# The scan's thirteen slots divided among KR, BK and Ar; loads issued three units ahead; M loaded through SyncE's queue

## The chip, the cores and the metric

One core of a Trainium2 chip runs the whole network once. The metric is the device time of one execution in microseconds; the median of the runs counts.

## The reference

Two layers, each half-SwiGLU, token mixer, half-SwiGLU, with adaptive RMS norms around them, on 512 latent tokens after 256 context tokens, width 1024, all in float32. The mixer of the first layer is HGRN2, that of the second RWKV-7. The change touches the scan of the RWKV-7 mixer alone, 16 heads of 64, in both directions:

```python
def step(s, inp):
    dec, kt, vt, kkt, bt = inp[:5]
    sa = jnp.einsum('bhvk,bhk->bhv', s, kkt)
    s = s * dec[:, :, None, :] - sa[..., None] * bt[:, :, None, :] + vt[..., None] * kt[:, :, None, :]
    y = jnp.einsum('bhvk,bhk->bhv', s, inp[5]) if with_out else None
    return s, y
...
s_fin, y = lax.scan(step, s0, xs, reverse=reverse)
```

The context is scanned first; the latent scan of the same direction starts from its final state.

## The kernel before, in words

The scan is done in chunks of 64 tokens. Work is cut into twelve units `(qd, g)`: four groups `qd` of four heads, and for each three stretches `g` of 256 tokens (0 is the context, 1 and 2 are the latent tokens), both directions at once. Each unit passes these steps:

- `prep_a` (L1225): loads `hw`, `kk` and `r` (tile KR, one per direction, L1243) and `ld` (L1246); decay matmuls `sw` (L1251), their cumulative sums `cum` (L1264), exponentials on ScalarE; VectorE scales KR in place (L1278) and makes BK from `ld` (L1281); TensorE multiplies BK with KR (L1304), VectorE masks the products into N and, where g is over 0, Ar (L1310); one N is transposed into NT (L1315), and N and NT are stored to a DRAM scratch `md` in eight pieces (L1318).
- `prep_m` (L1323): GpSimd loads M from `md` by its own queue (L1330), inverts 64 triangular 32 by 32 blocks in 30 steps of a product (L1336) and a sum (L1337), and stores the inverse to `me` (L1340).
- `prep_d` (L1344): SyncE loads the inverse in eight pieces into the diagonal blocks P (L1350).
- `prep_b` (L1352): SyncE loads VU (L1359); TensorE transposes BK into `bkt` (L1367, recorded on the helper's line L295), ScalarE copies it to BKT (L1368); matmuls W (L1380).
- `prep_c` (L1386): VectorE transposes P into PT (L1391); matmuls TT and Yo (L1409, L1411) join the diagonal blocks to inverses of 64 by 64.
- `scan` (L1430): four chunks in a row, each with matmuls kG from KR (L1447), `rhs` on VectorE (L1449), matmuls U (L1456), matmuls G from VU and BKT (L1466) and the new state G on VectorE (L1471, L1472), and where g is over 0 the output y from Ar and KR (L1482, L1484).
- `readout` after every third unit (L1497): norm, bonus and gate of two blocks of 128 channels, on TensorE, VectorE and ScalarE.

SBUF tiles of these steps come from rings: a tile takes a free slot of its tag, and what fills it waits until the last reader of the slot's former tile is through. KR, BK and Ar (two each in a unit) share thirteen slots in the pool B1; so do N, NT and M until the pool B2 is open. After that N, NT, M, BKT, W and PT share fifteen slots of B2 (`Q`, L1192).

The order of the instructions on each engine is fixed when the program is built: a scheduler simulates the engines and picks, of what is ready, the instruction that comes first in the program; `urgent` moves a step forward by 400 or 800 places. `rwkv_scan` writes the program's order with generators: the scan of unit i leads, and after each of its yields run three steps of the inversions, five of the preparation and 0.3 of a readout (RM, RP, RO). The preparation is the chain `SEQ = 'Adabc'` (L1556 to L1559): the first two steps of `prep_a` of unit i+2 (A), `prep_d` of i+1 (d), the rest of `prep_a` (a), `prep_b` and `prep_c` of i+1 (b, c). `prep_d` yields until the inversion of i+1 has been written down. Every load and store of the scan but those of M and `me` goes through SyncE's queue, which issues in order: a load that waits for its slot holds up everything behind it. Ahead of the loop a prologue runs beside the value projection (L1544): `prep_a` of unit 0, then the first inversion beside `NPRO` = 12 steps of `prep_a` of unit 1.

Of the kernel before, what the change touches and what calls it, by code (L numbers as in the profile page):

```python
# [9 lines left out]
F32 = mybir.dt.float32  # L10
# [13 lines left out]
I32 = mybir.dt.int32  # L24
RMS_EPS = 1e-6
GN_EPS = 64e-5
NQ1, NQ2 = 13, 15
RM, RP, RO, RV, RF = 3.0, 5.0, 0.3, 1.5, 1.3
NPRO = 12
ORDERED = {mybir.EngineType.PE, mybir.EngineType.DVE, mybir.EngineType.Activation}  # L30
LO = True
RX = 0.12
# [15 lines left out]
NBA, NBS, NB = 2, 4, 2  # L48
TCKW = dict(schedule_with_timeline_sim=True)
HP = 800, 400, 800  # L50
SEQ = 'Adabc'
Q1 = ("KR", "BK", "Ar")


V_NORM = 0
# [18 lines left out]
def trunk(ctx, tc, io, phases=None, dump=None):  # L74
    nc = tc.nc
    act, dve, pool, pe = nc.scalar, nc.vector, nc.gpsimd, nc.tensor
# [8 lines left out]
    def open_pool(name, side="left", **kw):  # L85
        cm = tc.tile_pool(name=name, bufs=1, side=side, reuse_waits="tile", **kw)
        opened[name] = cm
        return cm.__enter__()
# [45 lines left out]
    def urgent(gen, by):  # L134

        while True:
            with tc.high_priority(offset=by):
                x = next(gen, 0)
                if x == 0:
                    return  # L140
            yield x

    def both(*gens):

        gens = list(gens)
        while gens:
            for f in list(gens):
                if next(f, 0) == 0:
                    gens.remove(f)
                else:  # L150
                    yield
# [1029 lines left out]
    def rwkv_scan(l):  # L1181
        nonlocal work, wt, hpool, psw
        B1 = open_pool("B1")
# [6 lines left out]
        late = {}  # L1190

        def Q(name):  # L1192
            first = "B2" not in late or name in Q1
            return (B1 if first else late["B2"]).tile([128, 1024], F32, tag="Q", name=name, bufs=NQ1 if first else NQ2)

        turn = cycle(range(NB))

        def bank(name, tag="b"):

            own, n = {"a": ("a", NBA), "s": ("s", NBS), "b": ("b", 4 - NBA)}[tag]  # L1200
            in_s = tag == "s"
            if tag == "b" and "PS" in late and 4 - NBS and next(turn) == 0:
                in_s, n = True, 4 - NBS
            return (late["PS"] if in_s else PP).tile([128, 512], F32, tag=own, name=name, bufs=n)
# [20 lines left out]
        def prep_a(qd, g):  # L1225
# [7 lines left out]
            KR, BK, N, Ar = ([None, None] for _ in range(4))  # L1233
# [3 lines left out]
            for d in range(2):  # L1237
                t0 = starts(g)[d]
                kr = Q("KR")[:, :1024]
                KR[d] = kr.rearrange("p (s c n) -> p c s n", s=2, n=64)  # L1240
                src = lambda a: a[2 * qd:2 * qd + 2, :, t0:t0 + 256].rearrange("e p t -> p e t")
                for i, nm in enumerate(("kk", "r")[:1 + lat]):
                    nc.sync.dma_start(out=kr[:, 512 * i:512 * i + 512].rearrange("p (e t) -> p e t", e=2), in_=src(S[nm]))  # L1243
                ld = B1.tile([128, 2, 2, 256], F32, tag="L", name="ld", bufs=2)
                for i in range(2):
                    nc.sync.dma_start(out=ld[:, i], in_=src(S[f"bk{d}"][i]))  # L1246
                lds.append(ld)

                p = bank("sw", "a")
                for m in range(2):  # L1250
                    pe.matmul(p[:, 256 * m:256 * m + 256], hw[:, d, 128 * m:128 * m + 128],  # L1251
                              low[qd][:, d], start=True, stop=True)
                sg = B1.tile([128, 512], F32, tag="sg", name="sg", bufs=2)
                act.activation(sg, p, AF.Tanh, scale=0.5)
                dve.tensor_scalar(sg, sg, 0.5, 0.5, ALU.mult, ALU.add)
                sgs.append(sg)
                yield
# [12 lines left out]
            for d in range(2):  # L1270
# [5 lines left out]
                for i, o in ((0, ex), (1, inc))[:1 + lat]:  # L1276
                    x = KR[d][:, :, i]
# [38 lines left out]
            md = dram.tile([64, 32, 32], F32, tag="md", name="md", bufs=2)  # L1316
            for d, hp, b, l0, r0 in lanes:
                nc.sync.dma_start(out=md[l0:l0 + 8].rearrange("l s t -> s l t"),  # L1318
                                  in_=(N[0] if d == 0 else NT_)[r0:r0 + 32, 8 * hp:8 * hp + 8, 32 * b:32 * b + 32])
# [3 lines left out]
        def prep_m(qd, g):  # L1323

            while (qd, g) not in ready:
                yield
            md = ready[qd, g][-1]
            me = dram.tile([64, 32, 32], F32, tag="me", name="me", bufs=2)
            M = Q("M")[0:64, :1024].rearrange("l (s t) -> l s t", t=32)
            pool.dma_start(out=M, in_=md)  # L1330
            eng = ME
            mt = B1.tile([64, 256], F32, tag="mt", name="mt", bufs=2)
            for j in range(30, 0, -1):
                n = 31 - j
                t = mt[:, :j * n].rearrange("l (a b) -> l a b", b=n)
                eng.tensor_tensor(t, M[:, 0:j, j:j + 1].to_broadcast([64, j, n]), M[:, j:j + 1, j + 1:32].to_broadcast([64, j, n]), ALU.mult)  # L1336
                eng.tensor_tensor(M[:, 0:j, j + 1:32], M[:, 0:j, j + 1:32], t, ALU.add)  # L1337
                yield
            eng.memset(M.rearrange("l s t -> l (s t)")[:, 0:1024:33], 1.0)
            pool.dma_start(out=me, in_=M)  # L1340
            inverse[qd, g] = me
            yield
# [154 lines left out]
        def readout(qd, yb, sink):  # L1497

            def one(e):
                j, y = 2 * qd + e, yb[:, e]  # L1500
                ro = lambda n: late["B2"].tile([128, TL], F32, tag="ro", name=n, bufs=3) if qd < 3 else Q(n)[:, :TL]
                bv, g, q = ro("bvl"), ro("gl"), ro("q")
                nc.sync.dma_start(out=bv, in_=S["bv"][j])
                nc.sync.dma_start(out=g, in_=S["g"][j])
                yield
                p = bank("mean")
                pe.matmul(p, blk128, y, start=True, stop=True)
                dve.scalar_tensor_tensor(y, p, -1.0 / 64, y, ALU.mult, ALU.add)
                act.activation(q, y, AF.Square)
                yield  # L1510
                yield
                pq = bank("var")
                for c in range(4):
                    pe.matmul(pq[:, 2 * c:2 * c + 2], q[:, c * 128:c * 128 + 128], blk2, start=True, stop=True)
                rs = rsqrt(pq[:, :8], 8, 1.0 / 64, GN_EPS)
                act.activation(q.rearrange("p (c n) -> p c n", n=64), rs.unsqueeze(2).to_broadcast([128, 8, 64]), AF.Copy)
                yield
                yield
                pr = bank("rsb")
                for c in range(4):  # L1520
                    turned(pr[:, c * 128:c * 128 + 128], q[:, c * 128:c * 128 + 128], TR & 8)
                dve.tensor_tensor(y, y, pr, ALU.mult)
                act.activation(y, y, AF.Identity, scale=vcol(V_LNW, j), bias=vcol(V_LNB, j))
                yield
                dve.tensor_tensor(y, y, bv, ALU.add)
                dve.tensor_tensor(y, y, g, ALU.mult)
                sink(j, y)
                yield

            if qd < 3:  # L1530
                yield from one(0)
                yield from one(1)
            else:
                yield from both(one(0), one(1))
# [5 lines left out]
        none = out = iter(())  # L1540
        stage = lambda f, i: f(*todo[i]) if i < len(todo) else none
        second = prep_a(*todo[1])

        def prologue():  # L1544
            yield from prep_a(*todo[0])
            yield from both(prep_m(*todo[0]), islice(second, NPRO))

# [4 lines left out]
        for _ in both(second, chain(prep_d(*todo[0]), prep_b(*todo[0]), prep_c(*todo[0]))):  # L1552
            pass
        inversions = chain(*(prep_m(*k) for k in todo[1:]))
        for i, k in enumerate(todo):
            ahead = stage(prep_a, i + 2)  # L1556
            ahead = urgent(ahead, HP[1])
            parts = {"A": islice(ahead, 2), "a": ahead, "b": stage(prep_b, i + 1), "c": urgent(stage(prep_c, i + 1), HP[2]), "d": urgent(stage(prep_d, i + 1), HP[2])}
            prep = chain(*(parts[x] for x in SEQ))  # L1559
            due = [0.0] * 3  # L1560
            for _ in urgent(scan(*k, *ready.pop(k)), HP[0]):
                for n, (f, r) in enumerate(((inversions, RM), (prep, RP), (out, RO))):
                    due[n] += r
                    while due[n] >= 1.0:
                        due[n] -= 1.0
                        next(f, None)
            for _ in prep:
                next(inversions, None)
            if k[1] == 2:
                for _ in out:  # L1570
                    pass
                out = readout(k[0], state["y"], to_dram)
# [55 lines left out]
    if on("f00"):  # L1628
# [4 lines left out]
        prep = blocks(0, 0, T, True)  # L1633
# [30 lines left out]
    if on("f10"):  # L1664
# [3 lines left out]
        prep = blocks(1, 0, T)  # L1668
# [3 lines left out]
    if on("mix1"):  # L1672
        prep = squares(T)
# [88 lines left out]
```

## Time and profile before

| | us |
|---|---|
| median of 3 runs | 3894.08 (3892.76 to 3901.19) |
| the profiled execution | 3901.05 |
| its span | 3899.3 |
| TensorE busy | 3551.6 |
| VectorE busy | 2529.3 |
| GpSimd busy | 1382.0 |
| ScalarE busy | 1310.4 |

The profile is of one execution, and its times (us from the start of its span) are those of that execution. A group of instructions is shown by source line, engine, operation and tiles (out<-in). Engines are PE (TensorE matmuls), PEld (its weight loads), DVE (VectorE), ACT (ScalarE), POOL (GpSimd) and SP (SyncE); a q behind the name is the engine's queue, which issues DMAs. A float32 matmul appears as two instructions. What ended a wait is inferred from semaphores: where the engine named had long been done, it was another, often a DMA. The clock of TensorE is given as the granted share of 2.4 GHz, and it takes two levels, 1.00 and 0.50.

### The profile page before, as it was taken

Reading aid. Unit: us, or ns where it says so; the run is one execution under the profiler, and the core shown is the slowest. Engines: PE = TensorE matmul, PEld = TensorE weight load, DVE = VectorE, ACT = ScalarE, POOL = GpSimd, SP = SyncE. Lnnn points to the kernel's source line nnn. Section 1 sums busy time; section 2 is a strip of 40 time slices with the busy share of each in tenths; the row PEclk is TensorE's granted clock in tenths of the full one; section 3 lists DMA queues with packets and bytes.
Section 4 is the critical chain, followed back from the end, with each engine's and each line's share of the span. In section 5 each row is a group of like instructions: output and inputs, shape, how many; then the busy total and the mean of one; then the engine's idle time right before and its main releaser. Section 6 shows DMA issues by size and latency. Waiting matters only on the chain. (4 is left out here: it accounts for less than half of the span.)

```text
span 3899.3 us, 61645 instructions
## 1 busy us (share of the span) xinstructions
PE 3551.6 (91%) x24898; PEld 3115.9 (80%) x24898; DVE 2529.3 (65%) x4042; ACT 1310.4 (34%) x2024; POOL 1382.0 (35%) x1395
## 2 busy tenths in 40 slices
PE   5999998899999899999899999698978889889998
PEld 3898997688888688888799998576867777668887
DVE  6766667656666866666766675776444554468886
ACT  4332333232322432333532333354322222244343
POOL 4212213433433422122422221522366766523332
PEclk9999999999999899999999999798967776779999
DMA  5332331411112233333132332247633332233332
GB/s 186 115 96 88 97 98 44 114 43 44 39 44 66 66 113 103 103 110 113 52 95 82 90 95 78 66 155 240 164 88 81 83 82 63 61 106 91 94 93 81
DMA packets 517051, 362.52 MB, mean 93 GB/s; under 512 B 83517, under 2 KB 490333, under 8 KB 516766
## 3 DMA queue, kind: packets, MB, share of 16 engines
q1 hardware_dynamic: 513694, 350.19, 30.5%
q0 software_dynamic: 1920, 6.29, 0.7%
q8 instruction: 196, 3.21, 0.3%
q10 hardware_dynamic: 1152, 2.10, 0.2%
q14 instruction: 89, 0.73, 0.1%
HBM read 315.64 MB, written 42.87 MB: 92 GB/s over the span
## 5 line engine op out<-in xcount | busy, mean ns | idle before, releaser
L607 PE MATMUL po<-g,whi 128*128 128x512 f32 (+1 forms) x2464 | 593.4, 350 | 10.2 <-ACT g L211 10.2
L551 POOL TENSOR_TENSOR raw<-raw 128x512 f32<-128x512 f32 x88 | 124.9, 1419 | 1341.3 <-DMA raw<-in_ffn_w_in 772.4
L534 PE MATMUL c<-u,whi 128*128 128x386 f32 (+1 forms) x2112 | 524.5, 332 | 48.1 <-DVE uu L565 15.9
L526 ACT ACTIVATE whi<-raw 128x1024 fp32r<-128x1024 f32 x352 | 332.5, 950 | 570.4 <-PE po L607 306.9
L607 PEld LDWEIGHTS po<-g,whi 128*128 128x128 f32 x2464 | 406.2, 190 | 84.6 <-issue 11.4
L527 DVE TENSOR_TENSOR wlo<-raw,whi 128x1024 fp32r<-128x1024 f32 x352 | 416.4, 1187 | 32.3 <-ACT whi L526 30.6
L534 PEld LDWEIGHTS c<-u,whi 128*128 128x128 f32 x2112 | 371.6, 191 | 76.2 <-ACT u L446 25.1
L534 PE MATMUL a<-u,whi 128*128 128x386 f32 (+1 forms) x1408 | 347.4, 331 | 23.6 <-DVE u L428 17.2
L607 PE MATMUL po<-g,wlo 128*128 128x512 f32 (+1 forms) x1232 | 367.1, 348 | 0.0
L611 DVE SCALAR_TENSOR_TENSOR h<-po,mod,h 128x512 f32<-128x512 f32 (+1 forms) x384 | 228.3, 628 | 194.3 <-PE po L607 194.2
L534 PE MATMUL b<-u,whi 128*128 128x386 f32 (+1 forms) x1408 | 344.1, 329 | 2.3 <-ACT pp L562 1.4
L534 PE MATMUL c<-u,wlo 128*128 128x386 f32 (+1 forms) x1056 | 344.9, 327 | 0.0
L534 PEld LDWEIGHTS a<-u,whi 128*128 128x128 f32 x1408 | 251.8, 192 | 29.0 <-issue 18.4
L196 ACT ACTIVATE whi<-raw 128x1024 fp32r<-128x1024 f32 (+1 forms) x193 | 184.7, 959 | 266.8 <-PE c L534 108.5
L534 PEld LDWEIGHTS b<-u,whi 128*128 128x128 f32 x1408 | 246.5, 189 | 12.3 <-issue 6.6
L197 POOL TENSOR_TENSOR wlo<-raw,whi 128x1024 fp32r<-128x1024 f32 x48 | 127.0, 2647 | 302.7 <-ACT whi L196 284.1
L534 PE MATMUL a<-u,wlo 128*128 128x386 f32 (+1 forms) x704 | 233.1, 331 | 0.5 <-DVE wlo L527 0.5
L607 PEld LDWEIGHTS po<-g,wlo 128*128 128x128 f32 x1232 | 208.0, 190 | 29.8
L534 PE MATMUL b<-u,wlo 128*128 128x386 f32 (+1 forms) x704 | 229.2, 326 | 1.0 <-DVE wlo L527 1.0
L1336 POOL TENSOR_TENSOR mt<-M 64x168 f32<-64x168 f32 (+5 forms) x360 | 191.7, 533 | 67.6 <-DMA M<-md 41.2
L1337 POOL TENSOR_TENSOR M<-M,mt 64x168 f32<-64x168 f32 (+5 forms) x360 | 199.6, 555 | 26.4
L534 PEld LDWEIGHTS c<-u,wlo 128*128 128x128 f32 x1056 | 203.5, 193 | 0.0
(362 smaller groups left out, 7295.2 us busy)
## 6 DMA issues: line engine op xcount, KB each, us to landing
raw<-in_ffn_w_in SPq DMA_DIRECT2D x176, 512.0 KB
raw<-in_mod_w SPq DMA_DIRECT2D x144, 512.0 KB
raw<-in_ffn_w_out SPq DMA_DIRECT2D x80, 384.0 KB
raw<-in_hgrn_w_in SPq DMA_DIRECT2D x40, 512.0 KB
raw<-in_ffn_w_out SPq DMA_DIRECT2D x28, 512.0 KB
raw<-in_w_rkv SPq DMA_DIRECT2D x24, 512.0 KB
ld<-s_bk SPq DMA_DIRECT2D x48, 256.0 KB
s_bk<-knb SPq DMA_DIRECT2D x32, 192.0 KB
```

What stands on the lines that cost most here:

```text
L196: act.activation(hi[:, :m], raw[:, :m], AF.Copy)
L197: slots["lo"].tensor_tensor(lo[:, :m], raw[:, :m], hi[:, :m].bitcast(F32), ALU.subtract)
L526: act.activation(hi, x, AF.Copy)
L527: dve.tensor_tensor(lo, x, hi.bitcast(F32), ALU.subtract)
L534: pe.matmul(p[:, :q], a[:, c], x[k][:, b], start=first and k == 0 and i == 0, stop=k == 3 and i == 2, skip_group_check=not first)
L551: pool.tensor_tensor(S[:, lo], U[:, lo], U[:, hi], ALU.add)
L607: pe.matmul(p[v][:, :t1 - t0], wx[:, k, at:at + 128], x[:, e, t0:t1], start=k == 0 and i == 0, stop=k == nk - 1 and i == 2)
L611: dve.scalar_tensor_tensor(h[d][:, t0:t1], p[v][:, :t1 - t0], mods[l, sub, 2][:, d, v:v + 1], h[d][:, t0:t1], ALU.mult, ALU.add)
L1336: eng.tensor_tensor(t, M[:, 0:j, j:j + 1].to_broadcast([64, j, n]), M[:, j:j + 1, j + 1:32].to_broadcast([64, j, n]), ALU.mult)
L1337: eng.tensor_tensor(M[:, 0:j, j + 1:32], M[:, 0:j, j + 1:32], t, ALU.add)
```

## The change

The thirteen shared slots become three rings: 6 for KR, 3 for BK, 4 for Ar. Before the pool B2 is open, N takes slots of Ar's ring, NT and M of KR's. The loads of `prep_a` become a step of their own, ahead of the decay of both directions. In the loop of unit i the order becomes: loads of unit i+3, the decay steps of i+2, `prep_b` and `prep_d` of i+1, the rest of `prep_a` of i+2, `prep_c` of i+1. The prologue takes 10 steps of `prep_a` of unit 1 in place of 12, and the loads of unit 2 are written ahead of the loop. M is loaded by SyncE instead of GpSimd.

```diff
@@ -24,9 +24,9 @@
 I32 = mybir.dt.int32
 RMS_EPS = 1e-6
 GN_EPS = 64e-5
-NQ1, NQ2 = 13, 15
+RINGS, NQ2 = {"KR": 6, "BK": 3, "Ar": 4}, 15
 RM, RP, RO, RV, RF = 3.0, 5.0, 0.3, 1.5, 1.3
-NPRO = 12
+NPRO = 10
 ORDERED = {mybir.EngineType.PE, mybir.EngineType.DVE, mybir.EngineType.Activation}
 LO = True
 RX = 0.12
@@ -48,8 +48,6 @@
 NBA, NBS, NB = 2, 4, 2
 TCKW = dict(schedule_with_timeline_sim=True)
 HP = 800, 400, 800
-SEQ = 'Adabc'
-Q1 = ("KR", "BK", "Ar")
 
 
 V_NORM = 0
@@ -1190,8 +1188,13 @@
         late = {}
 
         def Q(name):
-            first = "B2" not in late or name in Q1
-            return (B1 if first else late["B2"]).tile([128, 1024], F32, tag="Q", name=name, bufs=NQ1 if first else NQ2)
+            if name not in RINGS:
+                if "B2" in late:
+                    return late["B2"].tile([128, 1024], F32, tag="Q", name=name, bufs=NQ2)
+                ring = "Ar" if name == "N" else "KR"
+            else:
+                ring = name
+            return B1.tile([128, 1024], F32, tag=ring, name=name, bufs=RINGS[ring])
 
         turn = cycle(range(NB))
 
@@ -1245,6 +1248,8 @@
                 for i in range(2):
                     nc.sync.dma_start(out=ld[:, i], in_=src(S[f"bk{d}"][i]))
                 lds.append(ld)
+            yield
+            for d in range(2):
 
                 p = bank("sw", "a")
                 for m in range(2):
@@ -1327,7 +1332,7 @@
             md = ready[qd, g][-1]
             me = dram.tile([64, 32, 32], F32, tag="me", name="me", bufs=2)
             M = Q("M")[0:64, :1024].rearrange("l (s t) -> l s t", t=32)
-            pool.dma_start(out=M, in_=md)
+            nc.sync.dma_start(out=M, in_=md)
             eng = ME
             mt = B1.tile([64, 256], F32, tag="mt", name="mt", bufs=2)
             for j in range(30, 0, -1):
@@ -1552,11 +1557,12 @@
         for _ in both(second, chain(prep_d(*todo[0]), prep_b(*todo[0]), prep_c(*todo[0]))):
             pass
         inversions = chain(*(prep_m(*k) for k in todo[1:]))
+        third = stage(prep_a, 2)
+        next(third)
         for i, k in enumerate(todo):
-            ahead = stage(prep_a, i + 2)
-            ahead = urgent(ahead, HP[1])
-            parts = {"A": islice(ahead, 2), "a": ahead, "b": stage(prep_b, i + 1), "c": urgent(stage(prep_c, i + 1), HP[2]), "d": urgent(stage(prep_d, i + 1), HP[2])}
-            prep = chain(*(parts[x] for x in SEQ))
+            ahead, third = urgent(third, HP[1]), stage(prep_a, i + 3)
+            b, c, d = stage(prep_b, i + 1), urgent(stage(prep_c, i + 1), HP[2]), urgent(stage(prep_d, i + 1), HP[2])
+            prep = chain(islice(third, 1), islice(ahead, 4), b, d, ahead, c)
             due = [0.0] * 3
             for _ in urgent(scan(*k, *ready.pop(k)), HP[0]):
                 for n, (f, r) in enumerate(((inversions, RM), (prep, RP), (out, RO))):
```

## Rows read from the trace of the kernel before

**Rows 1.** The profile page: the span, the engines' busy time, and the 40 slices of 97.5 us (the granted clock of TensorE alone).

```profile
span 3899.3 us, 61645 instructions
...
PE 3551.6 (91%) x24898; PEld 3115.9 (80%) x24898; DVE 2529.3 (65%) x4042; ACT 1310.4 (34%) x2024; POOL 1382.0 (35%) x1395
...
PEclk9999999999999899999999999798967776779999
```

**Rows 2.** Busy time by stretch of the scan stage: start and end in us, length, then busy us and count of instructions of each engine, the granted clock, the share of the DMA engines and GB/s. The first stretch runs from the load of M of unit 1 to that of unit 11, the second from there to the end of the stage; the third and the fourth lie inside the first, one at each clock.

```profile
2850.20:3344.60 494.40, 421.46 (x5612) 356.73 (x5608) 245.00 (x550) 124.13 (x302) 336.87 (x630) 0.73 0.30 76
3344.60:3435.00 90.40, 74.19 (x1046) 58.04 (x1046) 29.98 (x74) 19.83 (x47) 31.24 (x63) 0.70 0.28 79
3205.40:3239.60 34.20, 31.12 (x242) 26.40 (x241) 13.95 (x29) 6.99 (x16) 27.96 (x51) 0.50 0.21 55
3178.10:3205.40 27.30, 26.67 (x491) 23.42 (x487) 18.00 (x44) 10.78 (x25) 10.60 (x28) 1.00 0.49 119
```

**Rows 3.** The groups of GpSimd in 2850.2 to 3344.6: line, engine, operation, tiles, shapes, count | busy us, mean ns of one | idle us before them and what ended most of it.

```profile
L1337 POOL TENSOR_TENSOR M<-M,mt 64x30 f32<-64x30 f32 (+6 forms) x300 | 166.6, 556 | 21.9
L1336 POOL TENSOR_TENSOR mt<-M 64x30 f32<-64x30 f32 (+6 forms) x300 | 158.8, 530 | 54.1 <-DMA M<-md 32.2
L1340 POOL DMA_DIRECT2D me<-M x10 | 5.9, 587 | 2.7 <-POOL M L1337 2.7
L1330 POOL DMA_DIRECT2D M<-md x10 | 5.2, 525 | 109.2 <-DMA hw_s<-s_hw 44.1 <-PE cum L1264 43.2 <-ACT sg L1254 11.9
```

**Rows 4.** Waits of GpSimd in the same stretch: who waited for whom, us in total, times, longest.

```profile
POOL M L1330 <- PE cum L1264: 43.2, 2, 32.5
```

**Rows 5.** SyncE's queue in order of time: start, us, what it issued, count. The first two rows belong to units 6 and 7, the third is the load of KR of unit 8, then follow units 7, 8 and 9.

```profile
3132.22 3.75 SPq L1350 DMA_DIRECT2D P<-me  x8
3138.21 2.09 SPq L1318 DMA_DIRECT2D md<-NT  x4
...
3163.48 0.36 SPq L1243 DMA_DIRECT2D KR<-s_kk  x1
...
3187.12 3.91 SPq L1350 DMA_DIRECT2D P<-me  x8
3191.13 3.30 SPq L1318 DMA_DIRECT2D md<-NT  x4
...
3228.71 0.32 SPq L1318 DMA_DIRECT2D md<-NT  x1
3239.71 3.78 SPq L1350 DMA_DIRECT2D P<-me  x8
3243.53 1.44 SPq L1318 DMA_DIRECT2D md<-NT  x3
3245.07 0.40 SPq L1243 DMA_DIRECT2D KR<-s_kk  x1
```

**Rows 6.** VectorE in order of time; in brackets its idle time before the instruction and what ended it. The first group of rows is at unit 6's inverse, the next after the end of scan 5, the last at unit 8's inverse.

```profile
3135.03 0.71 DVE L1391 STREAM_TRANSPOSE PT<-P 128x512 f32<-128x512 f32 x1 [12.56 <-DMA P<-me]
...
3136.96 1.22 DVE L1315 STREAM_TRANSPOSE NT<-N 128x1024 f32<-128x1024 f32 x1
...
3163.90 1.76 DVE L1281 TENSOR_TENSOR BK<-ld,Ei 128x512 f32<-128x512 f32 x2 [0.32 <-PE y L1484]
...
3168.72 1.93 DVE L1278 TENSOR_TENSOR KR<-KR,E 128x512 f32<-128x512 f32 x2
...
3242.44 0.71 DVE L1391 STREAM_TRANSPOSE PT<-P 128x512 f32<-128x512 f32 x1 [12.67 <-DMA P<-me]
...
3247.97 0.69 DVE L1278 TENSOR_TENSOR KR<-KR,E 128x512 f32<-128x512 f32 x1 [3.83 <-DMA KR<-s_kk]
```

**Rows 7.** TensorE in order of time at the same two inverses.

```profile
3136.52 3.75 PE L1251 MATMUL sw<-w_s,hw_s 65*128 65x256 f32 x8 [9.52 <-DVE Ar L1310]
...
3243.52 2.10 PE L1264 MATMUL cum<-cst,sg 128*128 128x130 f32 x8 [3.92 <-DVE sg L1255]
```

**Rows 8.** Waits of TensorE in 2850.2 to 3344.6.

```profile
PE TT L1409 <- DVE PT L1391: 16.4, 2, 13.5
PE kG L1447 <- DVE G L1472: 10.3, 3, 6.4
...
PE sw L1251 <- DVE Ar L1310: 9.5, 1, 9.5
PE U L1456 <- DVE rhs L1449: 9.1, 5, 4.2
...
PE cum L1264 <- DVE sg L1255: 3.9, 1, 3.9
```

**Rows 9.** Waits of VectorE and of SyncE's queue in 2850.2 to 3344.6.

```profile
DVE PT L1391 <- DMA P<-me: 67.6, 9, 12.7
...
SPq L1350 <- DMA me<-M: 94.8, 9, 14.6
SPq L1243 <- PE y L1482: 50.6, 3, 18.5
SPq L1243 <- PE y L1484: 33.6, 3, 16.3
```

**Rows 10.** GpSimd in order of time, at the start of unit 11's inversion.

```profile
3344.65 0.52 POOL L1330 DMA_DIRECT2D M<-md  x1 [2.28 <-PE kG L1447]
3348.24 0.24 POOL L1336 TENSOR_TENSOR mt<-M 64x30 f32<-64x30 f32 x1 [3.07 <-DMA M<-md]
```

## The prediction

> **What bounds the kernel now.** I read the page first, then the stages, then who waits for whom in the one stage that the diff touches. The page says that TensorE is 91% busy over the span and that its clock sags late in it: the 30th to the 36th slice show 6 or 7, where most of the rest show 9 [rows 1]. That dip is the RWKV scan. From the load of M of unit 1 to that of unit 11, ten periods, it takes 494.4 us, 49.4 us a unit; the rest of the stage takes 90.4 [rows 2]. In the 494.4, TensorE is busy 421.5 us, so idle 72.9, at a mean clock of 0.73.
>
> GpSimd inverts one M a unit. Its time splits without a remainder that matters: steps 158.8 + 166.6, gaps between them 21.9 + (54.1 − 32.2) = 43.8, the landing of M 32.2, the store of me 5.9 + 2.7, the issue of M 5.2 [rows 3]. The wait ahead of that issue is 109.2, but 32.5 of it ended as the stretch began [rows 4]; 76.7 remain. The sum is 491.9 of 494.4. So 7.7 us a unit GpSimd waits for md, and 3.2 for M to land.
>
> Why md is late is in the queues. For unit 7 VectorE stands 12.56 us before PT of unit 6, then does the last N and NT of unit 7 [rows 6]; only then does SyncE store NT, at 3138.21 [rows 5]. For unit 9 the first NT store goes at 3228.71, the other three only behind unit 8's eight loads of P, at 3243.53 [rows 5]. Both P wait for the previous inverse: the inversion of one unit waits for the end of the last, and GpSimd, which could overlap, stands still. VectorE stands 67.6 us in the stretch before PT, and SyncE 94.8 for me [rows 9]. TensorE stops behind VectorE: 9.52 us after the PT of unit 6, 3.92 after that of unit 8 [rows 7].
>
> One step earlier is the ring. KR, BK and Ar of a unit are six tiles (four where g is 0), and thirteen slots hold two units and a bit. SyncE waits 50.6 + 33.6 = 84.2 us with a KR load for a scan's last readers [rows 9]; both BK products of unit 8 run at 3163.90, right after a y matmul released them, and KR's at 3168.72 [rows 6].
>
> **The change, part by part.** The arithmetic is the same; only slots, order and one queue move.
>
> *Rings.* BK has 3 slots: one is always free for the first direction of unit i+2, the second comes free with the first bkt transposes of unit i+1, which now stand ahead in the order. Ar has 4, two units of the three that have one, so it waits for nothing nearer than three units back. KR has 6, and KR of i+3 still needs KR of i, so the end of scan i. What goes away is BK's and Ar's part in the shared waiting. By itself it is worth nothing; it lets N, NT and md come ahead of the previous P.
>
> *Order.* Loads of i+3, then the decay of i+2, b and d of i+1, the rest of a, then c. No instruction is added. b moves ahead of a: its W and bkt matmuls delay a, at most by their own time, but TensorE does them anyway. In the prologue 10 steps instead of 12, where the loads are now a step of their own: three VectorE products fewer before the first inversion. Nearest price, 0.9 us each (1.76 for two [rows 6]): 0 to 3 us of cost. I take 0, since they then lie beside that inversion on GpSimd.
>
> *M through SyncE.* Twelve issues leave GpSimd (5.2 us for ten [rows 3]), twelve are added to SyncE at about 0.4 each [rows 5]. A KR load of the same size, the nearest row, is issued at 3245.07 and used at 3247.97 [rows 5, 6], 2.9 us, against 3.6 for M on GpSimd [rows 10]. If M comes late that is 0.7 us a unit; if md is early, the landing lies beside the previous inversion and all 3.7 go. New is that SyncE waits for md's landing with M at its head: behind it stand P, md and the next loads. That is about 2 us a unit on a queue that now waits 94.8 us for me alone, so I price it at 0, upper end 10 × 2 = 20 us.
>
> *The sum.* If GpSimd alone set the pace, it could drop 76.7 + 32.2 + 5.2 = 114 us. It can't all show: TensorE's 421.5 busy us stand beside it. So the gain is the TensorE idle time that hangs on the late inverse. Of its waits [rows 8] those for PT (16.4), G (10.3), Ar (9.5), rhs (9.1) and sg (3.9) are the ones that follow VectorE's stand before PT, as rows 6 and 7 show twice: 49.2 us. Not every one of the smaller waits is followed to its PT; that is my choice of upper bound. From it I leave 13.5, the longest wait for PT, which falls in the first unit, where no slot was short: 35.7. In the tail, M of unit 11 is issued 2.28 us after GpSimd came free [rows 10], and that goes if M is already there: 2.3. Together 38 us. Lower bound of the gain: zero, if the new order makes the same stands elsewhere. Upper bound at this clock: all 72.9 of idle time plus 2.3, 75 us. I take 38, since the rest of the idle time belongs to the readout and to the scan's own chain, which the change leaves.
>
> The profiled execution took 3901.05 us, span 3899.3; the median of the three runs is 3894.08, 7 us less. 3901.05 − 38 = 3863; against the median, **3856**. A measurement of this kernel tells some 0.2%, 8 us, from no change.
>
> **A rule against taking TensorE for the bound.** TensorE's busy time here is 85% of the stretch, and that of its weight loads 356.7 us, 72% [rows 2]. The Trainium skill (Perfetto Trace Analysis, Identifying the Most-Contended Engine) says that matmul occupancy misjudges the distance to the roofline, since matmuls are pipelined, and that the share of weight loads should be read instead. By that rule TensorE's floor would be 356.7, GpSimd would set the pace, and the gain would be the 114 and not 38. The trace speaks for the busy time: at clock 0.50 it runs 31.1 of 34.2 us and does 242 matmuls, at 1.00 26.7 of 27.3 and does 491 [rows 2]; it is full at either level, and at the lower it does half.
>
> **Rivals.**
> *GpSimd sets the pace.* With fewer stands the clock of 2.4 GHz is granted longer, TensorE's floor sinks under GpSimd's 369.2 + 8.6 = 378 us. Then 494.4 falls to about 395 (some landings stay): −99, **3795**. For it: the rates of the two levels. Against: the clock was 0.50 for 34 us in which TensorE was 91% busy [rows 2], so being busy did not raise it. 13%.
> *The ring closes on the scan as before.* KR still waits for scan i's end, so "three units ahead" is an order on paper only. Unit 8: KR issued at 3163.48, last md store ended at 3194.43 [rows 5], 31 us, of which the wait behind P takes 3.9. If only that is saved in the three turns of the ring, 12 us, and b ahead of a costs as much again: 0 to −8, **3890**. 14%.
> *SyncE's queue takes the wait over.* All twelve units' KR loads now wait for a scan's end; six waits of before took 84.2 us, 14 each [rows 9]. If the loads are placed ahead of md and M in the queue, GpSimd waits the 14, not the 7.7 of today: 10 × (14 − 7.7) = 63 worse, less the 32.2 of M's landing: +31, **3925**. It decides once a KR load stands with M behind it for more than 7.7 + 3.2 = 11 us a unit. For it: two of today's stands took 18.5 and 16.3. Against: the KR loads of before did the same beside md's stores. 20%.
>
> **How the numbers follow.** Forecast (3830 to 3885) 52%, the rivals 13, 14 and 20, 1 for anything else. Faster by over 0.2%, under 3886: 52 + 13 + 2 of the ring's 14 = 67%. Within: the other 12. Slower: 21. The range leaves out the lower half of the first rival and the upper half of the last: 3800 to 3920.
>
> **What would show it.** Right: GpSimd's wait before M's first product under 3 us a unit; VectorE's 67.6 before PT under 35; md's NT stores ahead of the previous P in SyncE's queue; the stretch of ten periods at 455 to 460 us; TensorE busy above 90% of it. Wrong: SyncE's waits for y over 140 us with M behind them; or PT again ahead of NT on VectorE; or the clock well above 0.73, which means the first rival.

## The result, and the profile after

The changed kernel is slower: 3943.18 us median (3936.02 to 3952.25, four runs) against 3896.6 for the kernel before (3892.76 to 3901.19), a ratio of 1.012 [1.0095, 1.0146]. The prediction was 3856, and the time lies above its range. In the changed kernel the lines L1232 to L1246 stand three further down, those from L1251 on five, and the helpers' two further up.

The page after: TensorE does the same busy work in a longer span.

```profile
span 3950.5 us, 61576 instructions
...
PE 3545.1 (90%) x24898; PEld 3108.4 (79%) x24898; DVE 2529.1 (64%) x4042; ACT 1312.2 (33%) x2024; POOL 1376.9 (35%) x1383
...
PEclk9999999999999999999999998898868686779999
```

The windows of the changed kernel, from the load of M of unit 1 to that of unit 11 and from there to the end of the stage, with the columns of [rows 2]:

```profile
2857.65:3393.39 535.74, 418.81 (x5704) 351.02 (x5706) 249.64 (x555) 126.60 (x305) 330.71 (x620) 0.75 0.28 71
3393.39:3484.00 90.61, 68.01 (x938) 52.98 (x934) 27.20 (x71) 17.92 (x43) 31.00 (x62) 0.63 0.24 70
```

The ten periods grew by 41.3 us, from 494.4 [rows 2]. TensorE's busy time there did not grow (418.8 against 421.5) and the clock is no lower (0.75 against 0.73). So between these two profiles the loss is idle time, 116.9 against 72.9 us. The tail is as long as before. Another 7.4 us lie ahead of the stretch: it begins at 2857.65, not 2850.20. The two profiled executions lie 51.2 us apart, the medians 46.6.

GpSimd's groups in the stretch:

```profile
L1342 POOL TENSOR_TENSOR M<-M,mt 64x30 f32<-64x30 f32 (+7 forms) x300 | 166.4, 556 | 21.2
L1341 POOL TENSOR_TENSOR mt<-M 64x30 f32<-64x30 f32 (+7 forms) x300 | 158.5, 530 | 210.1 <-DMA M<-md 148.1 <-PE G L1471 33.1 <-DVE gs L1298 7.8
L1345 POOL DMA_DIRECT2D me<-M x10 | 5.8, 579 | 2.7 <-POOL M L1342 2.7
```

The steps cost what they did [rows 3], and the wait has moved from the issue of M to its first product. What counts is the gap from the last sum of one inversion to the first product of the next. Read from GpSimd's timeline, the ten gaps (units 2 to 11) add up to 121.6 us before and 160.1 after, 38.5 more. Unit 2 has none in either kernel; the others, in us:

| unit | 3 | 4 | 5 | 6 | 7 | 8 | 9 | 10 | 11 |
|---|---|---|---|---|---|---|---|---|---|
| before | 14.7 | 15.6 | 5.3 | 16.0 | 16.9 | 16.1 | 14.1 | 16.3 | 6.8 |
| after | 34.0 | 13.8 | 15.3 | 15.8 | 19.4 | 8.9 | 15.6 | 20.5 | 16.8 |

Units 3, 5 and 11 carry 39.3 us; the others nearly cancel.

Who waits, for [rows 8] and [rows 9]:

```profile
PE TT L1414 <- DVE PT L1396: 90.2, 9, 20.9
DVE PT L1396 <- DMA P<-me: 92.2, 13, 19.3
SPq L1355 <- DMA me<-M: 98.7, 7, 20.0
SPq L1246 <- PE y L1489: 31.9, 6, 13.6
SPq L1335 <- DMA md<-NT: 6.8, 9, 1.3
SPq L1249 <- DVE BK L1286: 70.1, 11, 15.8
SPq L1249 <- DVE gs L1298: 18.8, 4, 9.4
```

The same stands before the load of `ld` in the kernel before:

```profile
SPq L1246 <- DVE BK L1281: 25.0, 13, 6.0
SPq L1246 <- DVE gs L1293: 8.6, 2, 5.8
```

TensorE stands 90.2 us at TT for PT, where it stood 16.4. SyncE's waits for y fell from 84.2 to 31.9; its stands before `ld` grew from 33.6 to 88.9. But md and M did not stand behind those loads: in eight of the nine units 3 to 11 the first store of NT is issued within 0.1 us of NT's end (in unit 4 it stands behind P), and M 1.8 to 3.0 us after the last store. So the third rival's queue did not form. One unit shows how the order of VectorE holds md back. At the inverse of unit 8, VectorE in order of time:

```profile
3260.60 0.36 DVE L286 SCALAR_TENSOR_TENSOR rsy<-rsa,rsy 128x8 f32<-128x8 f32 x1
3273.68 0.71 DVE L1396 STREAM_TRANSPOSE PT<-P 128x512 f32<-128x512 f32 x1 [12.72 <-DMA P<-me]
3274.31 0.72 DVE L1315 TENSOR_TENSOR N<-A,cst 128x256 f32<-128x256 f32 x2
3275.12 1.25 DVE L1320 STREAM_TRANSPOSE NT<-N 128x1024 f32<-128x1024 f32 x1
```

SyncE's queue, TensorE and GpSimd at the same place:

```profile
3271.03 3.75 SPq L1355 DMA_DIRECT2D P<-me  x8
3276.40 2.27 SPq L1323 DMA_DIRECT2D md<-NT  x4
3280.11 0.47 SPq L1335 DMA_DIRECT2D M<-md  x1
```

```profile
3274.45 0.32 PE L1414 MATMUL TT<-PT,N 32*32 32x32 f32 x4 [14.75 <-DVE PT L1396]
```

```profile
3268.11 0.58 POOL L1345 DMA_DIRECT2D me<-M  x1 [0.29 <-POOL M L1342]
3283.43 0.24 POOL L1341 TENSOR_TENSOR mt<-M 64x30 f32<-64x30 f32 x1 [14.74 <-DMA M<-md]
```

Unit 9's last two N stand behind unit 8's PT on VectorE, so md and M come after unit 8's inverse, and GpSimd waits 14.7 us between two inversions while TensorE stands 14.75. Before, TensorE stood 3.92 us at this place [rows 7], but GpSimd's gap was 14.1 there too: NT was ready in time, and three of its stores stood behind the loads of P on SyncE's queue [rows 5]. Before, NT of a unit came ahead of the former PT in seven of the nine units 3 to 11; now in two. All eight stores came ahead of the loads of P in two (5 and 11), where the gap was 5.3 and 6.8; now in one (8), at 8.9. So units 5 and 11 lose 10 us each by the order, and most of the others had little to lose.

The largest loss, 19.3 us, is at unit 3. There NT comes 19.5 us behind the first PT of unit 2, since on TensorE the last N products of unit 3 stand behind TT, which waits for that PT, and behind matmuls of the scan:

```profile
2943.99 0.71 DVE L1396 STREAM_TRANSPOSE PT<-P 128x512 f32<-128x512 f32 x1 [6.62 <-DMA P<-me]
2963.51 1.25 DVE L1320 STREAM_TRANSPOSE NT<-N 128x1024 f32<-128x1024 f32 x1
```

```profile
2944.85 0.32 PE L1414 MATMUL TT<-PT,N 32*32 32x32 f32 x4 [5.60 <-DVE PT L1396]
2960.66 1.97 PE L1309 MATMUL A<-KR,BK 64*128 64x64 f32 x16
```

### The profile page after: what moved, and what is told of

Same layout as the page of the kernel before. It is cut to its first block, busy times and chain, and to the rows that moved or that the text cites. A ratio compares the mean times of both kernels' runs of the same rounds, so it can differ in the third digit from the quotient of the medians.

```text
span 3950.5 us, 61576 instructions
## 1 busy us (share of the span) xinstructions
PE 3545.1 (90%) x24898; PEld 3108.4 (79%) x24898; DVE 2529.1 (64%) x4042; ACT 1312.2 (33%) x2024; POOL 1376.9 (35%) x1383
## 4 chain that ended last, share of the span: by engine, by line
PE 30%; POOL 9%; DVE 5%; issue 5%; DMA 1%; ACT 1%; SPq 0%; POOLq 0%; DVEq 0%; ACTq 0%
PE po L605 8%; PE c L532 6%; POOL M L1342 4%; POOL mt L1341 4%; PE a L532 4%; PE b L532 3%; PE v L220 1%; PE k L220 1%; PE o L220 1%; PE A L1309 1%; DVE mx L958 1%; DVE wlo L525 1%; PE a L1083 0%; DMA tv<-s_xv 0%; PE modp L250 0%
## 5 line engine op out<-in xcount | busy, mean ns | idle before, releaser
L532 PE MATMUL c<-u,whi 128*128 128x386 f32 (+1 forms) x2112 | 523.7, 332 | 50.0 <-DVE uu L563 16.1
L525 DVE TENSOR_TENSOR wlo<-raw,whi 128x1024 fp32r<-128x1024 f32 x352 | 412.3, 1175 | 33.4 <-ACT whi L524 31.9
L1341 POOL TENSOR_TENSOR mt<-M 64x234 f32<-64x234 f32 (+6 forms) x360 | 190.7, 531 | 288.9 <-DMA M<-md 222.3
L605 PEld LDWEIGHTS po<-g,wlo 128*128 128x128 f32 x1232 | 207.6, 190 | 29.8
L1342 POOL TENSOR_TENSOR M<-M,mt 64x234 f32<-64x234 f32 (+6 forms) x360 | 200.9, 559 | 25.8
```

The costliest lines, as they stand in the source:

```text
L525: dve.tensor_tensor(lo, x, hi.bitcast(F32), ALU.subtract)
L532: pe.matmul(p[:, :q], a[:, c], x[k][:, b], start=first and k == 0 and i == 0, stop=k == 3 and i == 2, skip_group_check=not first)
L605: pe.matmul(p[v][:, :t1 - t0], wx[:, k, at:at + 128], x[:, e, t0:t1], start=k == 0 and i == 0, stop=k == nk - 1 and i == 2)
```

## The experiments

Three theories. **A**: a serial loop. PT and TT stand, in the fixed order of VectorE and TensorE, ahead of the N and NT that the next inversion needs; so inverse, P, PT, N, NT, md, M and the next inverse follow one another. **B**: M, md and the KR loads wait for one another in SyncE's queue. **C**: KR in a ring of its own waits for the end of the scan three units back.

The table is made as above: the stretch from M's load of unit 1 to that of unit 11, TensorE's idle time in it (length less busy), and the ten gaps of GpSimd, in us. Differences below are against the kernel before on the same chip (medians of 3896.5 to 3899.1). The last three columns are of one profiled execution, and that is not always near the median: after's is the highest of its four, 3952.3; e14's and e16's are the lowest of theirs, 3908.3 and 3883.2, so these rows flatter them.

| | median | ratio [95%] | stretch | idle | gaps |
|---|---|---|---|---|---|
| before | 3896.6 | | 494.4 | 72.9 | 121.6 |
| after | 3943.2 | 1.0120 [1.0095, 1.0146] | 535.7 | 116.9 | 160.1 |
| e1 | 3925.8 | 1.0066 [1.0049, 1.0083] | 517.0 | 109.8 | 145.5 |
| e2 | 3905.1 | 1.0022 [1.0012, 1.0031] | 504.7 | 73.4 | 132.3 |
| e3 | 3932.1 | 1.0089 [1.0072, 1.0106] | 515.5 | 106.3 | 144.8 |
| e4 | 3974.1 | 1.0192 [1.0173, 1.0212] | 568.9 | 167.7 | 196.5 |
| e5 | 3925.0 | 1.0071 [1.0055, 1.0088] | 508.9 | 89.8 | 135.0 |
| e6 | 3899.4 | 1.0000 [0.9990, 1.0011] | 490.7 | 97.2 | 111.4 |
| e7 | 3908.5 | 1.0025 [1.0014, 1.0036] | 491.4 | 101.4 | 122.5 |
| e8 | 3913.4 | 1.0038 [1.0021, 1.0055] | 493.4 | 95.2 | 124.6 |
| e9 | 3900.5 | 1.0008 [0.9999, 1.0018] | 495.7 | 88.3 | 119.9 |
| e10 | 3921.8 | 1.0055 [1.0038, 1.0072] | 496.6 | 102.8 | 128.2 |
| e11 | 3930.7 | 1.0085 [1.0067, 1.0103] | 517.3 | 108.1 | 148.4 |
| e12 | 3925.7 | 1.0073 [1.0058, 1.0088] | 521.0 | 108.2 | 151.1 |
| e13 | 3883.4 | 0.9962 [0.9947, 0.9978] | 486.4 | 83.0 | 298.6 |
| e14 | 3932.3 | 1.0080 [1.0051, 1.0108] | 506.0 | 96.1 | 306.9 |
| e15 | 3901.3 | 1.0009 [0.9999, 1.0019] | 498.4 | 83.5 | 119.9 |
| e16 | 3893.4 | 0.9992 [0.9977, 1.0006] | 482.1 | 92.3 | 106.3 |
| e17 | 3786.0 | 0.9712 [0.9691, 0.9734] | 395.1 | 23.6 | 189.1 |
| e18 | 3831.5 | 0.9844 [0.9816, 0.9872] | 441.8 | 37.6 | 240.6 |

TensorE's idle time alone does not tell the length of the stretch: e6 and e7 stand 97.2 and 101.4 us, more than the kernel before, and their stretch is 3 to 4 us shorter, at a granted clock of 0.77 and 0.78 instead of 0.73, with 393.5 and 390.0 us of busy time for nearly the same matmuls.

### M's queue: e1 and e2

e1 is the changed kernel with M back on GpSimd's queue, e2 the kernel before with M on SyncE's:

```diff
-            nc.sync.dma_start(out=M, in_=md)
+            pool.dma_start(out=M, in_=md)
```

> The changed kernel with one part undone: M is loaded through GpSimd's own queue again. Theory A (the loss is in the written order: the joins PT and TT of a unit stand at the head of VectorE and TensorE before its inverse has come): the load's queue hardly matters, 3930 to 3960 us. Theory B (SyncE's queue holds M and md behind loads that wait for a scan's end): most of the loss goes, 3890 to 3910. Theory C (KR's ring of six): 3930 to 3960, like A.

> The kernel before with one part of the change alone: M through SyncE's queue. Theory A: within 10 us of the kernel before. Theory B: 20 to 45 us slower. Theory C: within 10 us.

M on SyncE's queue costs 7.2 us in the old order (3905.1 against 3897.9) and 17.4 in the new one (3943.2 against 3925.8). That is less than B says, and not all of it is the queue's: the edit also makes VectorE's order anew. In e1 NT is ahead of the former PT in six of nine units instead of two, and the gaps are 145.5; in the changed kernel itself SyncE's queue held md back in one unit of nine, as shown above.

### The rings and the order apart: e3 and e4

e3 puts the three rings into the old order (with NPRO 9, for the prologue to fit); e4 keeps the new order and M on SyncE, with thirteen shared slots:

```diff
-NQ1, NQ2 = 13, 15
+RINGS, NQ2 = {"KR": 6, "BK": 3, "Ar": 4}, 15
...
-NPRO = 12
+NPRO = 9
```

> The kernel before with the three rings alone (6, 3, 4 slots; the prologue takes 9 of its old steps, since the tenth takes a slot of BK that comes free only later); old order, M on GpSimd. Theory A: within 15 us of the kernel before, or faster. Theory B: within 15 us. Theory C (both KR of unit i+3 now wait for the end of scan i): 25 to 50 us slower.

> The changed kernel with the thirteen shared slots of before: new order, loads three ahead, M on SyncE. Theory A: as slow as the change, 3930 to 3960. Theory B: also 3930 to 3960 (M is on SyncE). Theory C: back near 3900.

The rings, with the shorter prologue that they need, cost 34.2 us in the old order. The gap of unit 3 is 14.5 us here, and 14.1 to 14.7 in every run of the old order with the whole inversion but e9; in those of the new order it is 33 to 40, in e8 21.6. So this part of the loss comes with the new order (its prologue included), not with the rings or M's queue. All three theories missed e4. With shared slots the new order is worst of all, 76.2: KR then loads 55 us ahead of the end of the scan three units back (mean of units 3 to 11) and takes the slots that the unit before still needs for BK, whose first product comes 26 us after that end (2 us ahead of it in the kernel before). So the new order needs the rings, and the rings with NPRO 9 cost in themselves.

### One ring at a time: e5, e6 and e7

```diff
-NQ1, NQ2 = 13, 15
+RINGS, NQ2 = {"KR": ("KR", 6), "BK": ("BA", 7), "Ar": ("BA", 7)}, 15
```

e5 is this in the old order, e6 the same with `{"KR": ("KB", 9), "BK": ("KB", 9), "Ar": ("Ar", 4)}`, both with NPRO 9; e7 is the kernel before with NPRO 9 alone.

> The kernel before with KR on a ring of its own of 6 slots, BK and Ar sharing the other 7; 9 prologue steps, as in the run of the rings alone (which was 34 us slower). If KR's ring is what costs (both KR of unit i+3 wait for the end of scan i), 20 to 40 us slower than the kernel before; if it is BK's three slots, within 10 us; if any division costs because slots lie idle that another tile could use, about half, 10 to 25 us.

> The kernel before with Ar on a ring of its own of 4 slots, KR and BK sharing the other 9; 9 prologue steps. If KR's ring is what costs, within 10 us of the kernel before; if BK's three slots, within 10 us too; if any division costs, 10 to 25 us slower.

> The kernel before with the prologue taking 9 steps of the second unit in place of 12, the other edit that the run of the rings alone had to make. Every theory but one: within 8 us of the kernel before. If the prologue is what cost the 34 us: 25 us or more slower.

NPRO 9 costs 9.4 us by itself, more than the 8 expected and behind the stretch, which is 3 us shorter; KR's ring adds 16.5 to that; Ar's ring takes 9.1 off again. KR's first load of a unit came 15.2 us (mean) ahead of the end of the scan three units back; with six slots of its own it comes 3.1 ahead, and in the changed kernel 2.6. That is C in place and sign, but how the later load costs time is not shown. md's last store is issued 34.8 us after that scan's end in e5, 37.2 in e7, and against e7 TensorE's idle time in e5 is 11.6 us less. The stretch is 17.5 us longer because busy time is 29.1 more, at a lower granted clock (e5, then e7):

```profile
2852.44:3361.32 508.88, 419.08 (x5561) 353.50 (x5560) 247.39 (x547) 122.11 (x299) 339.47 (x630) 0.72 0.30 74
```

```profile
2851.04:3342.46 491.42, 390.03 (x5534) 329.04 (x5534) 239.28 (x547) 122.26 (x297) 334.65 (x631) 0.78 0.30 76
```

### The priority: e8 and e15

`HP` holds how far the scan, the rest of `prep_a`, and `prep_c` with `prep_d` are moved forward. e8 is the changed kernel, e15 the kernel before, with

```diff
-HP = 800, 400, 800
+HP = 800, 800, 400
```

> The changed kernel with the steps of prep_a moved forward by 800 places, like the scan, and prep_d and prep_c by 400 in place of 800. Theory A (the loss is that PT and TT of one unit stand at the head of VectorE and TensorE ahead of N and NT of the next): NT comes ahead of PT, GpSimd's wait before M's first product falls from 17.8 us a unit to under 10, and the time to 3900 or less. If the slots decide, it stays within 15 us of the change.

> The kernel before with the priority of the rest of prep_a raised from 400 to 800 and that of prep_c and prep_d lowered from 800 to 400: N and NT of the next unit ahead of PT. Serial loop: in the old order NT is ahead of PT in seven of nine units already, so there is little left to gain, 0 to -12 us, 3886 to 3898, and the gaps of GpSimd fall a little. If the gain of 30 us that the same edit made in the changed kernel is a general one and not the undoing of the change's own damage: -25 us or more.

In the changed kernel this gives back 29.8 of the 46.6 us, between what the two theories expected; in the kernel before it gives nothing (+4.8). NT is ahead of PT again in six of nine units, the gaps are back at 124.6, and the window and the wait for PT, 90.2 before the edit, read:

```profile
2853.94:3347.34 493.40, 398.18 (x5578) 334.84 (x5573) 243.55 (x549) 122.99 (x296) 331.03 (x619) 0.75 0.30 76
```

```profile
PE TT L1414 <- DVE PT L1396: 45.3, 7, 25.1
```

So with rings and queues left alone, a priority that puts N and NT first takes most of the loss back, as A says, and it is damage of the change, not a gain to be had anywhere. How often NT leads is not the whole of it: e1 has six of nine as well, and gives back 17.4.

### md past the loads of P: e9 and e10

md's stores on ScalarE's queue, so that P can't stand ahead of them; e9 in the kernel before, e10 in the changed one:

```diff
-                nc.sync.dma_start(out=md[l0:l0 + 8]...
+                nc.scalar.dma_start(out=md[l0:l0 + 8]...
```

> The kernel before with the eight stores to md of each unit issued by ScalarE's queue in place of SyncE's. Theory D (GpSimd's gap between two inversions is about 15 us wherever md of a unit is stored behind the previous inverse's loads of P on SyncE or behind PT on VectorE, and about 5 where md is stored first): in five of nine units NT was ready before PT and only SyncE's order held md, so the mean gap falls from 13.5 us to under 10 and the time by 15 to 45 us. If TensorE alone sets the pace, the time stays within 10 us.

> The changed kernel with the stores to md on ScalarE's queue. Theory D: here only two of nine units had NT ready before PT, so little is won, 0 to 15 us against the change.

e9 is a miss: no gain. The gap of unit 3 fell from 14.7 to 5.4 us, that of unit 10 rose from 16.3 to 24.9. In the changed kernel the same edit gives 21.4, more than the 0 to 15 expected.

### A seventh KR, a fourth BK: e11 and e12

e11 is the changed kernel with another slot for KR, e12 with another for BK; to make room, a ring elsewhere in the stage (`bol`) has one buffer instead of two and `NQ2` is 14:

```diff
-RINGS, NQ2 = {"KR": 6, "BK": 3, "Ar": 4}, 15
+RINGS, NQ2 = {"KR": 7, "BK": 3, "Ar": 4}, 14
```

> The changed kernel with a seventh slot for KR (14 slots for the three rings, 14 in place of 15 for the others, one buffer less for a small tile of the prologue). If KR's ring of six costs because the first direction of KR, too, waits for the end of the scan three units back: the first KR load comes 10 us or more ahead of that end as in the kernel before, and the time falls by 10 to 30 us against the change. If it isn't KR, within 10 us of it.

> The changed kernel with a fourth slot for BK, memory as in the run with a seventh for KR. If the second direction's wait for a free slot of BK costs: that direction of BK comes at least 5 us earlier against the scan's end and the time falls by 10 to 30 us. If KR decides, within 10 us of the change.

12.5 and 17.5 us better. But with seven KR the first load comes 54 us ahead of the scan's end instead of 2.6, and md's last store is where it was, 42.6 us behind it (41.5). So an earlier load does not bring md earlier, and the 12.5 us did not come that way: the edit also made the order anew (NT ahead in five of nine units, in e12 in four). In e12 the second direction of BK comes 10.8 us earlier against the scan's end, as expected, but md's last store only 0.9.

### The inversion itself: e13 and e14, e17 and e18

e13 (before) and e14 (after) leave half of the steps out:

```diff
-            for j in range(30, 0, -1):
+            for j in range(30, 15, -1):
```

> The kernel before with 15 of the 30 steps of every inversion left out (those with j from 15 down), so an inversion takes GpSimd about 18.7 us instead of 37.3; nothing is exact in the output, and all transfers, waits and orders stay as they are. Theory of the serial loop (inverse to P to PT to N and NT of the next unit to md to M to inverse): the stretch of ten periods is paced by the inversion and the gap behind it, so it loses most of its 73 to 77 us of TensorE idle time, between 30 and 60 us; a time of 3838 to 3868. Theory that the slots of KR and BK on the scan's end set the pace: the loads stay where they are against the scan, at most 15 us are gained, 3883 or more.

> The changed kernel with the same 15 steps left out. Serial loop: the change only lengthened that loop, so with the inversion short enough the difference to the run with the old order (now 46.6 us) falls to 15 us or less, here 3840 to 3880. Theory that the rings on the scan's end cost by themselves: the 46.6 us stay within 12 us of where they are, so some 35 us or more above the run with the old order. Theory of M behind SyncE's queue: 8 to 17 us of difference stay.

Both are misses for A: the kernel before gains 13.1 us only, and 48.9 stay between the two. But the program's order is made from simulated times, and with the shorter inversion it came out anew: in both, PT now stands ahead of NT in all nine units. e17 (before) and e18 (after) therefore take the program as it was scheduled, and only shrink the operands of the inversion's products and sums to one row afterwards. No instruction moves on any engine.

```diff
+    for block in nc.m.functions[0].blocks:
+        for k, i in enumerate(block.instructions):
+            if ... "prep_m" in str(i.debug.bass_funcname):
...
+                    block.instructions[k] = i.__replace__(ins=[cut(x, n[0]) for x in i.ins], outs=[cut(x, n[0]) for x in i.outs])
```

> The kernel before with each engine's order of instructions exactly as it was (e13 and e14 left steps out, and the scheduler then ordered TensorE's and VectorE's work anew, which clouds them): only the products and sums of the inversion work on one row instead of j rows, so 56 of the 60 instructions of an inversion take about 0.24 us instead of 0.4 to 0.76, and an inversion about 14 us instead of 37. The result is not the inverse. Serial loop: TensorE's waits that hang on the late inverse go, 35 to 70 us, so 3830 to 3865. Slots on the scan's end: 15 us or less, 3883 or more.

> The changed kernel with the same cut, each engine's order as it was in it. Serial loop: TensorE's 90 us before TT fall under 30 and the 46.6 us between the two kernels to 15 or less, so 3845 to 3880. Slots on the scan's end, or TensorE's new order by itself: 35 us or more stay between this run and the other. Something between, 15 to 35, means that the loop carries a part and the rest comes before the inversion.

The windows of e13, e17 and e18:

```profile
2837.21:3323.56 486.35, 403.35 (x5577) 343.07 (x5576) 228.51 (x550) 120.28 (x297) 177.76 (x330) 0.73 0.31 78
```

```profile
2838.08:3233.13 395.05, 371.46 (x5562) 315.30 (x5560) 212.47 (x547) 120.47 (x293) 164.27 (x630) 0.84 0.38 95
```

```profile
2846.12:3287.93 441.81, 404.18 (x5670) 338.53 (x5665) 216.10 (x554) 123.86 (x299) 154.07 (x620) 0.79 0.35 86
```

And what is left in e18 of TensorE's wait for PT:

```profile
PE TT L1414 <- DVE PT L1396: 19.8, 5, 14.3
```

An inversion's steps take 19.8 us in e17, not the 14 expected. The kernel before gains 111.8 us, more than I expected; the changed one 111.7. TensorE's idle time falls by 49.3 us (72.9 to 23.6) and by 79.3 (116.9 to 37.6), so of the 44.0 us of idle time that the change added, 14.0 are left. So in both kernels the inversion is on the path that sets the pace, and in idle time most of the difference goes with it, as A says. In time my expectation for e18 fell, and A with it: 45.5 us stay between the kernels, what the expectation gave to the slots or to TensorE's new order. They are made up otherwise: of the stretch, 46.8 us longer in e18, 14.0 are idle and 32.7 busy time, with the same work: the granted clock is 0.84 in e17 and 0.79 in e18. Why it rose less in e18 the runs do not tell, so it is not shown that the change's 46.6 us hang on the inverse.

e13 and e17 do the same transfers with inversions of the same length (18.6 and 19.8 us of steps) and lie 97 us apart; the edits differ in the order, and the granted clock came out at 0.73 and 0.84.

### Ar's ring with the whole prologue: e16

e6 with NPRO 12:

> The kernel before with a ring of 4 for Ar and 9 slots shared by KR and BK, with the prologue of 12 steps kept (the same rings with 9 steps measured 3899.4, and 9 steps alone cost 9.5 us). If the two add up: 3890, -9 us. If 9 steps only cost where KR shares its slots with Ar: 3899, no difference.

No difference from the kernel before is shown. None of the runs beats both kernels with the computation whole.

## Why the prediction was wrong

- **What bounds the kernel: right.** The late inverse stops TensorE. I counted 49.2 us of its waits as hanging on it; with the inversion shortened in the same order (e17), its idle time fell by 49.3. That the two agree so closely is partly luck: the five waits that I had counted fell by 40.0 (to the three below; the other two are gone), and the rest came from waits that I had left out.

```profile
PE TT L1409 <- DVE PT L1391: 6.0, 1, 6.0
PE sw L1251 <- DVE Ar L1310: 1.8, 1, 1.8
PE U L1456 <- DVE rhs L1449: 1.4, 2, 0.9
```

- **The step that failed is *Rings***: "it lets N, NT and md come ahead of the previous P". It did not. I read the order off the program's text and did not ask where the scheduler would then put PT and TT. N's products on TensorE for a unit's second direction begin 23.9 us (mean) after the end of the scan three units back, 17.6 before, so its N and NT are late, and PT and TT, moved forward by 800, come first. Of nine units, NT was ahead of PT in seven before and is in two now; md was stored whole ahead of P in two, and is in one. So there was something to win, gaps of 14 to 17 us in seven units, and instead the two short gaps went and that of unit 3 grew by 19.3. The term of −35.7 came out as 44.0 us more idle time. The wrong sign that I had named, PT again ahead of NT on VectorE, is what the trace shows.
- ***Rings*, KR**: I wrote that KR of i+3 needs the end of scan i, and priced that at nothing. It had been a wait for some units [rows 9]; in a ring of six it is one for both directions of every unit. With its own ring the first load comes 12 us later (15.2 ahead of the scan's end before, 3.1 in e5), and the time with that ring is 16.5 us longer; the way from the one to the other is open. The second rival had this place, with a price of 0 to −8: wrong sign.
- ***M through SyncE***, taken at 0 with an upper end of 20: 7.2 in the old order, 17.4 in the new, with whatever the new orders of these runs did. The 0.7 us that I gave SyncE's queue for its landing is not there: M takes 3.2 to 4.5 us from issue to first product on it, 3.2 to 4.7 on GpSimd's. The third rival's 3925 is nearest to the time, but its mechanism, KR waits of over 140 us with M behind them, is not in the trace: they fell to 31.9. The prologue's cost, taken at 0 with an upper end of 3, is not borne out either: the stretch begins 7.4 us later. No run tests that alone.
- **The clock at a fixed 0.73**: no error for this change (0.75), but wrong as a rule. From one low stretch with TensorE 91% busy I concluded that being busy did not raise the clock. (The rates were misread as well: 242 matmuls in 31.1 busy us against 491 in 26.7 are 42%, not half, and the kinds of matmul need not be the same.) In e17, with TensorE busy 371.46 of 395.05 us, it is 0.84, and the clock gives 50.0 us of busy time besides the 49.3 of idle time. The Trainium skill (Perfetto Trace Analysis, Identifying the Most-Contended Engine) warns against taking matmul occupancy for the distance to the roofline. In e17 TensorE is 94% busy, and its stretch is 99.4 us shorter, with a busy time 50.0 us under the 421.5 that I had taken for a floor; so my upper bound of 75 us was none. e17 also takes some 173 us off GpSimd's steps, so it does not test the 114 us.
- **What stays open** is how the 46.6 us divide among the parts. M's queue, KR's ring and the order of PT do not add up, since each edit makes TensorE's order anew, and two orders with the same transfers and inversions of the same length lay 97 us apart. That every edit by which the changed kernel's order was made anew, but e4, gains 11 to 30 us says that a part of the loss may belong to this one order. And why the granted clock of the stretch lies between 0.72 and 0.84 in kernels with nearly the same matmuls, while its busy time lies between 371 and 431 us, no run tells.

## What to carry to other kernels

Before issuing loads earlier, follow the loop that sets the pace through every in-order engine: if the producer of the next round stands behind the consumer of this one on a single engine, earlier loads change nothing there, as e11's seventh KR slot showed for md. Giving each tile its own ring trades a shared wait for a fixed one; write down which last reader frees each slot, for each unit and direction. Where a scheduler derives the order from simulated times, test a cause with the order held, as in e17 and e18; an edit that makes the order anew tests two things at once.

## What the runs showed of the hardware

- GpSimd's products and sums, cut to 2 to 30 elements in a partition, take about 255 ns where the means over 30 to 240 elements were 530 and 556 [rows 3], so nearly half of a step does not go with its elements. GpSimd's groups in e17's window:

```profile
L1337 POOL TENSOR_TENSOR M<-M,mt 64x30 f32<-64x30 f32 (+6 forms) x300 | 76.5, 256 | 21.8
L1336 POOL TENSOR_TENSOR mt<-M 64x30 f32<-64x30 f32 (+6 forms) x300 | 76.2, 255 | 55.7 <-DMA M<-md 33.8
```

- In two kernels with the same TensorE work and order (before and e17), the mean granted clock of the scan rose from 0.73 to 0.84 once 49 us of its waits were gone. More waiting does not always go with a lower clock: in e7, in another order, TensorE stands 28.5 us longer than before and the granted clock is 0.78.
